# A hybrid encoder layer with seven more fused weight pairs, x loaded once, and x added to the output by accumulating transfers

## The chip, the cores and the metric

The kernel runs on one core of a Trainium2 chip. Its engines are named as in the profile: PE multiplies matrices (PEld is its weight load), DVE works on vectors, ACT does activations and copies, POOL and SP issue transfers here. The metric is the device time of one execution in microseconds; lower is better.

## The reference, cut to what matters

One layer on x of 256 rows and 4096 columns, float32. Its two large products are with w_in (4096 x 14336) and w_out (4096 x 4096).

```python
xn = rms_norm(x, norm_g[l])
h = jnp.einsum('bsd,de->bse', xn, w_in[l])
c_val, c_glu, c_gate, q, k, v, a_gate = jnp.split(h, split_pts, axis=-1)
conv_out = conformer_conv(c_val, c_glu, conv_w[l], conv_b[l], conv_ln_g[l], conv_ln_b[l])
conv_out = conv_out * jax.nn.silu(c_gate)
q = rms_norm(q.reshape(B, S, ATTN_HEADS, HEAD_DIM), q_norm_g[l])
k = rms_norm(k.reshape(B, S, ATTN_HEADS, HEAD_DIM), k_norm_g[l])
attn = longnet_mixture(q, k, v, rel_bias).astype(x.dtype).reshape(B, S, ATTN_WIDTH)
attn_out = attn * jax.nn.silu(a_gate)
mixed = jnp.concatenate([conv_out, attn_out], axis=-1)
x = x + jnp.einsum('bse,ed->bsd', mixed, w_out[l])
```

`conformer_conv` is a gated product, a 31-tap convolution along the rows, a LayerNorm over channels and a swish. The attention has 16 heads of 128 over the 256 rows.

## The kernel before, in words

**Groups and slots.** The weights are read once, in 18 groups of 1024 columns: groups 0 to 13 multiply the normalised x with w_in (four for the convolution, two for its gate, eight for attention), groups 14 to 17 multiply the mixed rows with w_out. A group goes through its 4096 weight rows in 16 pairs of 128, one pair in a slot; `ORDERS` gives the order of the pairs in a group. A pair's 128 x 2048 numbers (1 MB) arrive in one of three `raw` buffers (`load_pair`, on SP's queue).

**Split products.** Both operands are split into a high and a low part of a faster format. ACT makes the high part by a cast, DVE the low part by a subtraction, and PE forms high x high, low x high and high x low. A pair consists of 2 x 2 blocks on each side, so a plain pair (`split_plain`, `plain`) has 8 block products of 3 matmuls, 24 matmuls.

**Fused pairs.** The pairs listed in `FUSED` use a scheme of 7 block products, so 21 matmuls (`split_fused`, `fused`). They need sums of weight blocks, made by DVE in place in `raw` (L1083, L1095, L1096), and sums of the rows' blocks (`block_sums`), made once a pair of rows and kept. Their products go to four more accumulators, m1, m5, m6 and m7, which `add_more` combines behind the group's last fused pair; L1291 to L1309 are its additions in the output groups. The lists give 5, 7, 7, 7, 7 and 6 fused pairs in groups 2 to 7, four in group 14 and seven each in groups 15 to 17.

**Accumulators.** There are two sets of four, `acc` and `side`, which change roles from group to group: a group's m1 to m7 take the set in which the group before kept its outputs.

**Order of the work.** The program is written out by a planner. Every engine runs its instructions in order. `before` issues the split steps of the coming weights as far as there is room (four tiles of 2048 columns, and four of 1024 around fused pairs, `W_SLOTS` and `W_MORE`). Everything else stands in lanes of generators (convolution, attention heads, LayerNorm, the split of the mixed rows), and `pump` lets a lane issue its next step while a budget of DVE and ACT time, credited as PE's matmuls are issued, is above zero. The last slot of a group is plain and sums accumulator by accumulator (`plain_last`: four high matmuls, then two low ones, for each); in slots ahead of it sixteen matmuls with the high half come before the low half.

**The normalisation.** Group 0 multiplies the raw x times the gain g; its root mean square is applied when its outputs leave the accumulators (L876, L878), and group 1 does the same (L901, L907). For it x is loaded a second time in another layout in eight chunks (`load_x`), squared on ACT with a sum along the row (`square_x`), and the reciprocal root (`finish_rstd`) goes through DRAM to become a row that all partitions hold. During group 1 the columns of x are loaded a third time, scaled by that row (L294), cast (L301), subtracted (L303) and from group 2 on used.

**The outputs.** In an output group x is loaded in slot 7 (`xr`, L1156), DVE adds the combined products and then the four accumulators to it (L855), and SP stores it (L857), all at the end of the same group.

Of the kernel before, what the change touches and what calls it, by code (L numbers as in the profile page):

```python
# [132 lines left out]
def layer_kernel(  # L133
# [37 lines left out]
    def rsqrt(src, shape, mul, eps, name, wait=True):  # L171
# [3 lines left out]
        v = sb.tile(shape, F32, tag=tag, bufs=bufs, name=name + "v")  # L175
        r = sb.tile(shape, F32, tag=tag, bufs=bufs, name=name + "r")
        t = sb.tile(shape, F32, tag=tag, bufs=bufs, name=name + "t")
# [74 lines left out]
    def new_split(k, nm):  # L252
        h = sb.tile([P, S], F32R, tag="xh", bufs=KT, name=f"{nm}h{k}")
        l = sb.tile([P, S], F32R, tag="xl", bufs=KT, name=f"{nm}l{k}")
        return h, l

    ss = const.tile([P, 2, 8], F32, name="ss")
    xT, x_chunks = {}, {}

    def load_xT(k0, n, queue):  # L260

        t = t4(f"xT{k0}")
        queue.dma_start(
            t[:, :n, :].rearrange("p a b -> p (a b)"),
            x_cols[:, KT + S * k0 : KT + S * (k0 + n)],
        )
        for i in range(n):
            xT[k0 + i] = t[:, i, :]

    def load_x(c):  # L270
        t = t4(f"x{c}").rearrange("p a b -> p (a b)").rearrange("p (s d) -> p s d", s=2)
        nc.sync.dma_start(t, xs[:, :, 512 * c : 512 * c + 512])
        x_chunks[c] = t

    def square_x(c, s):
        junk = t2(f"junk{c}_{s}")
        nc.scalar.activation(
            junk, x_chunks[c][:, s, :], AF.Square, accum_out=ss[:, s, c : c + 1]
        )

    def split_x(k):
        h, l = new_split(k, "x")
        src = xT.pop(k)
# [7 lines left out]
    def split_xn(k):  # L291

        src = xT[k]
        nc.vector.scalar_tensor_tensor(  # L294
# [16 lines left out]

    split_gens = deque()

    def split_more():

        for gen in list(split_gens)[:4]:
            cost = next(gen, None)
# [1125 lines left out]
```

## Time and profile before

| | before |
|---|---|
| median of 3 runs | 1565.15 us (1565.12 to 1566.41) |
| profiled execution | 1565.9 us, its span 1564.1 us |
| busy: PE, DVE, ACT, POOL | 1559.1, 1335.1, 971.0, 98.9 us |
| matmul records | 6874 |
| group 0 | 0 to 93.8 us |
| group 1 | 93.8 to 180.8 us |
| groups 15 and 16 | 1313.0 to 1395.3 and 1395.3 to 1477.6 us |
| last matmul starts | 1559.9 us |

The span runs from the first to the last instruction. In a row of a view by groups stand the line, the engine, the operation, the tiles written and read, the count, busy time and mean, and after the bar the time for which the engine idled just ahead of these instructions, with what ended it. A busy PE is not PE at its peak: a matmul record lasts 389 ns while the next one starts 227 ns after it.

### The profile page before, as it was taken

The numbers are of one execution on the slowest core, as the hardware profiler recorded it, in microseconds if no ns is written. First come the engines' busy times: TensorE is split into PE (matmuls) and PEld (weight loads), VectorE is DVE, ScalarE is ACT, GpSimd is POOL, SyncE is SP. The second block draws the span as 40 slices with busy tenths as digits, with TensorE's granted clock in tenths as the row PEclk, the third lists the DMA queues.
The fourth block names the chain that finished last, engine by engine and source line by source line (L and its number), as shares of the span: only waits on it lengthen the run. The fifth ranks groups of instructions, "written<-read, shape, count | busy, mean of one in ns | idle before, by whom it ended". The sixth has DMA issues, their size and how long they took to land.

```text
span 1564.1 us, 18620 instructions
## 1 busy us (share of the span) xinstructions
PE 1559.1 (100%) x6874; PEld 1290.6 (83%) x6874; DVE 1335.1 (85%) x1495; ACT 971.0 (62%) x1503; POOL 98.9 (6%) x184
## 2 busy tenths in 40 slices
PE   9999999999999999999999999999999999999999
PEld 7888888888888888888888888888888888888887
DVE  5658898999999999898798898789575888999988
ACT  6755555565556566667776786776557754555453
POOL 0000000000000000001130022021010400000000
PEclk9999999999999999999999999999999999999999
DMA  9768565655656555659686488567674965666663
GB/s 373 293 220 298 189 224 206 226 191 201 233 212 228 199 207 213 216 190 284 219 279 216 174 256 269 194 206 272 220 239 161 282 233 201 239 240 242 223 248 122
DMA packets 64523, 357.22 MB, mean 228 GB/s; under 512 B 9104, under 2 KB 11920, under 8 KB 27824
## 3 DMA queue, kind: packets, MB, share of 16 engines
q1 hardware_dynamic: 54096, 326.38, 59.1%
q0 software_dynamic: 10048, 29.37, 6.3%
q8 instruction: 54, 0.88, 0.2%
q10 hardware_dynamic: 288, 0.28, 0.1%
q14 instruction: 37, 0.30, 0.1%
HBM read 337.09 MB, written 18.91 MB: 228 GB/s over the span
## 4 chain that ended last, share of the span: by engine, by line
PE 99%; DMA 0%; DVE 0%; SPq 0%; ACT 0%; DVEq 0%; issue 0%
PE c L1253 44%; PE c L1255 22%; PE m L1224 6%; PE c L1269 4%; PE m L1226 3%; PE c L1271 2%; PE c L1114 2%; PE c L1112 2%; PE c L1224 2%; PE c L1113 2%; PE acc L956 2%; PE acc L953 2%; PE acc L954 2%; PE m L1114 1%; PE c L1226 1%; PE m L1113 1%
## 5 line engine op out<-in xcount | busy, mean ns | idle before, releaser
L1057 DVE TENSOR_TENSOR wl<-raw,wh 128x2048 fp32r<-128x2048 f32 x208 | 475.7, 2289 | 150.2 <-ACT wh L1051 140.9
L1051 ACT CAST wh<-raw 128x1024 fp32r<-128x1024 f32 x416 | 414.9, 1048 | 222.1 <-PE c L1255 134.7
L1253 PE MATMUL c<-wh,nh 128*128 128x512 f32 x1128 | 439.6, 390 | 0.0
L1255 PE MATMUL c<-wh,nl 128*128 128x512 f32 x1128 | 438.9, 389 | 0.0
L1074 ACT CAST t<-raw 128x1024 fp32r<-128x1024 f32 x128 | 134.9, 1054 | 253.9 <-DVE raw L1083 190.5
L1253 PE MATMUL c<-wl,nh 128*128 128x512 f32 x1128 | 280.5, 391 | 0.0
L1253 PEld LDWEIGHTS c<-wh,nh 128*128 128x128 f32 x1128 | 211.7, 188 | 44.0
L1255 PEld LDWEIGHTS c<-wh,nl 128*128 128x128 f32 x1128 | 211.7, 188 | 44.0
L1253 PEld LDWEIGHTS c<-wl,nh 128*128 128x128 f32 x1128 | 211.8, 188 | 43.9
L1075 DVE TENSOR_TENSOR t<-raw,t 128x1024 fp32r<-128x1024 f32 x128 | 156.2, 1221 | 3.6 <-ACT t L1074 0.3
L508 ACT ACTIVATE cp<-a,wT 128x241 f32<-128x241 f32 (+8 forms) x252 | 105.6, 490 | 6.4 <-DVE cT L537 6.3
L1253 PE MATMUL c<-wh,mh 128*128 128x512 f32 x280 | 109.1, 390 | 0.0
L1255 PE MATMUL c<-wh,ml 128*128 128x512 f32 x280 | 108.9, 389 | 0.0
L546 DVE SCALAR_TENSOR_TENSOR cT<-a,wT,cT 128x255 f32<-128x255 f32 (+7 forms) x228 | 95.1, 473 | 0.5
L1083 DVE TENSOR_TENSOR raw<-raw 128x1024 f32<-128x1024 f32 x64 | 78.4, 1225 | 2.2
L1075 DVE TENSOR_TENSOR b<-raw,b 128x1024 fp32r<-128x1024 f32 x64 | 78.0, 1218 | 0.3
L537 DVE TENSOR_TENSOR cT<-cT,cp 128x964 f32<-128x964 f32 (+8 forms) x63 | 73.8, 1172 | 2.8 <-DVE cT L537 0.5
L1253 PE MATMUL c<-wl,mh 128*128 128x512 f32 x280 | 69.2, 389 | 0.0
L1074 ACT CAST b<-raw 128x1024 fp32r<-128x1024 f32 x64 | 67.0, 1047 | 1.9 <-DMA raw<-in_w_dram 1.2
L1255 PEld LDWEIGHTS c<-wh,ml 128*128 128x128 f32 x280 | 52.6, 188 | 10.9
L1253 PEld LDWEIGHTS c<-wl,mh 128*128 128x128 f32 x280 | 52.6, 188 | 10.9
L1253 PEld LDWEIGHTS c<-wh,mh 128*128 128x128 f32 x280 | 52.6, 188 | 10.9
(343 smaller groups left out, 2275.0 us busy)
## 6 DMA issues: line engine op xcount, KB each, us to landing
raw<-in_w_dram SPq DMA_DIRECT2D x286, 1024.0 KB, 4.9
xT<-in_x_cols_dram SPq DMA_DIRECT2D x15, 512.0 KB, 7.3
x<-in_x_dram SPq DMA_DIRECT2D x8, 512.0 KB, 8.2
xr<-in_x_dram SPq DMA_DIRECT2D x8, 512.0 KB, 6.7
out_dram<-xr SPq DMA_DIRECT2D x15, 256.0 KB, 7.4
T<-bias_dram SPq DMA_DIRECT2D x16, 192.0 KB, 5.6
raw<-in_w_dram SPq DMA_DIRECT2D x3, 512.0 KB, 6.7
turn_qk0d<-turn_qk POOLq DMA_DIRECT2D x2, 512.0 KB, 5.1
```

The source lines that it names most:

```text
L508: nc.scalar.activation(cp[:, t, lo:hi], a[:, t, lo + sh : hi + sh], AF.Copy, scale=wT[:, 4 * cb + t, k : k + 1],)
L537: nc.vector.tensor_add(c[:, :, lo:hi], c[:, :, lo:hi], cp[:, :, lo:hi])
L546: nc.vector.scalar_tensor_tensor(c[:, t, lo:hi], a[:, t, lo + sh : hi + sh], wT[:, 4 * cb + t, k : k + 1], c[:, t, lo:hi], op0=ALU.mult, o ...
L1051: nc.scalar.copy(h, raw_tiles[u][:, k])
L1057: nc.vector.tensor_sub(l, src, h.bitcast(F32))
L1074: nc.scalar.copy(h, src)
L1075: nc.vector.tensor_sub(l, src, h.bitcast(F32))
L1083: nc.vector.tensor_add(r[:, 0:4:3, :], r[:, 0:3:2, :], twice(r[:, 3, :]))
L1224: nc.tensor.matmul(acc, ah, b, start=begin, stop=end)
L1253: nc.tensor.matmul(acc, a[s][0], b[e], start=begin, stop=False)
L1255: nc.tensor.matmul(acc, a[s][1], b[e], start=False, stop=False)
L1269: nc.tensor.matmul(acc, a[s][0], b[e], start=False, stop=end)
```

## The change: what it does

**More fused pairs.** Group 1 gets three (slots 6, 8 and 12), group 2 six, group 7 seven, groups 15 and 16 eight each with a new slot order. In these two the slots run plain, plain, fused, plain, fused, plain, fused, fused, plain, fused, plain, fused, plain, fused, fused, plain. Group 17 keeps its order and its seven.

**x loaded once.** The columns of x stay in eight tiles. ACT squares them whole, DVE adds the squares up, and PE sums over partitions by a product with a tile of ones, which leaves the row in every partition; two one-column products give the same numbers as columns. The pairs of rows are scaled, cast and subtracted (now two blocks in one instruction) from step n = 19 of group 0 on, as far as the budget allows, and group 1 works on normalised rows like the others. The block sums for pairs that group 1 does not fuse are made in group 2.

**Wider or moved operations.** The convolution's centre tap goes from DVE to ACT (`center_gen`). The gate product and the split of the mixed rows work on wider tiles.

**Outputs of groups 14 to 16.** `add_more` combines the fused products in a tile of its own, as in the input groups, with four DVE additions instead of eight; then POOL issues two transfers that add x to that tile as they land. The four accumulators are added, and the result is stored, after slot 0 of the next group (`late_out`). Group 17 keeps the old way.

```diff
+LATE = 0
...
-XN_LOAD = {1 + (5 * c + 1) // 2: c for c in range(8)}
-XN_SQUARE = {n + 5 + s: (c, s) for n, c in XN_LOAD.items() for s in range(2)}
+
+X_LOAD = {0: 12, 1: 16, 3: 20, 5: 24, 6: 28}
+X_SQUARE = {4: 4, 5: 0, 6: 8, 7: 12, 8: 16, 9: 20, 10: 24, 11: 28}
+
+N_SPLIT, N_WAIT = 10, 3
...
-FUSED_IN = range(2, 8)
-N_FUSED = dict(zip(FUSED_IN, (5, 7, 7, 7, 7, 6)))
-FUSED = [(2, 4, 6, 8, 10, 12, 13)[: N_FUSED.get(g, 0)] for g in range(N_IN)]
-SUMS = max(FUSED)
-FUSED += [range(4)] + 3 * [range(7)]
+FUSED_IN = range(1, 8)
+SUMS = (2, 4, 6, 8, 10, 12, 13)
+FUSED = [SUMS if g in FUSED_IN else () for g in range(N_IN)]
+FUSED[1], FUSED[2] = (6, 8, 12), SUMS[1:]
+FUSED += [range(4), range(8), range(8), range(7)]
 ORDERS = N_IN * [range(16)]
 ORDERS += [(4, 5, 8, 9, 10, 11, 12, 13, 0, 14, 1, 15, 2, 6, 3, 7)]
-ORDERS += 3 * [(8, 9, 0, 10, 1, 11, 2, 12, 3, 13, 4, 14, 5, 6, 15, 7)]
+ORDERS += 2 * [(8, 9, 0, 10, 1, 11, 2, 3, 12, 4, 13, 5, 14, 6, 7, 15)]
+ORDERS += [(8, 9, 0, 10, 1, 11, 2, 12, 3, 13, 4, 14, 5, 6, 15, 7)]
...
+    def new_pair(j, nm):
+
+        return [
+            sb.tile([P, 2, S], F32R, tag=f"x{part}", bufs=n_pairs, name=f"{nm}{part}{j}")
+            for part in "hl"
+        ]
...
+    x_tiles = {}
+
+    def sum_squares():
+
+        total = t4("squares")
+        for i, k0 in enumerate(X_SQUARE.values()):
+            t = t4(f"sq{k0}") if i else total
+            if k0:
+                nc.scalar.activation(t, x_tiles[k0], AF.Square)
+            else:
+                nc.scalar.activation(t[:, 0, :], xT[0], AF.Square)
+                nc.scalar.activation(t[:, 1:, :], x_tiles[0][:, :3, :], AF.Square)
+            spend(0, 1055)
+            yield
+            if i:
+                nc.vector.tensor_add(total, total, t)
+                spend(1225)
+        total = flat(total)
+        for n in (512, 256):
+            nc.vector.tensor_add(total[:, :n], total[:, :n], total[:, n : 2 * n])
+            spend(160 + n)
+        yield
+        yield
+        yield from finish_rstd(total[:, :S])
...
+    def split_xn(j):
+
+        steps = 2 * j, 2 * j + 1
+        for k in steps:
+            nc.vector.scalar_tensor_tensor(
+                xT[k], xT[k], g_cols[:, k : k + 1], state["rstd_row"], op0=ALU.mult, op1=ALU.mult
+            )
+            yield 480
...
+        h, l = new_pair(j, "n")
+        for i, k in enumerate(steps):
+            nc.scalar.copy(h[:, i, :], xT[k])
+        yield 0, 800
+        for _ in range(N_WAIT):
+            yield 0
+        if both(j):
+            nc.vector.tensor_sub(l, both(j), h.bitcast(F32))
+            yield 690
+        else:
+            for i, k in enumerate(steps):
+                nc.vector.tensor_sub(l[:, i, :], xT[k], h[:, i, :].bitcast(F32))
+            yield 830
+        for i, k in enumerate(steps):
+            xnh[k], xnl[k] = h[:, i, :], l[:, i, :]
+        if j in FUSED[FUSED_IN[0]]:
+            yield from x_sums(j)
...
+    def split_more(forced=False):
+
+        for gen in list(split_gens)[: 2 if forced else N_SPLIT]:
+            if left[0] <= 0 and not forced:
+                break
             cost = next(gen, None)
             if cost is None:
                 split_gens.remove(gen)
             else:
                 spend(*(cost if isinstance(cost, tuple) else (cost,)))
+
+    def x_sums(j):
+        yield from block_sums(
+            j, src_of=xT, parts=(xnh, xnl), out=xsum, name="xs", small=j in SUMS[5:]
+        )
...
+    def finish_rstd(total):
+
+        pm = side("rms")
+        nc.tensor.matmul(pm[:, :S], ones, total, start=True, stop=True)
+        for i in range(2):
+            nc.tensor.matmul(
+                pm[:, S + i : S + i + 1], total[:, P * i : P * i + P], ones[:, 0:1],
+                start=True, stop=True,
+            )
+        yield
+        steps = rsqrt(pm[:, : S + 2], [P, S + 2], CW / D, NORM_EPS, "rx", wait=False)
+        cost = next(steps)
+        state["held"] -= 1
+        yield cost
+        r = yield from steps
+        state["rstd_row"] = r[:, :S]
+        state["rstd"] = [r[:, S + i : S + i + 1] for i in range(2)]
...
+    def center_gen(cb):
+
         while cb not in aT:
             yield
         a = aT[cb]
         c = t4(f"cT{cb}")
         for t in range(4):
             ch = 4 * cb + t
...
+            nc.scalar.activation(
+                c[:, t, :], a[:, t, :], AF.Identity, bias=col("conv_b", ch),
...
+    xr_tiles, late_out = {}, deque()
...
-        elif g == 1 and e == 1:
-            tile_, first = plain_tiles[(g, 0)]
-            t = first[:, s, :]
-            nc.vector.scalar_tensor_tensor(
-                t, acc, state["rstd"][s], t, op0=ALU.mult, op1=ALU.mult
-            )
-            spend(745)
         else:
-            scale = state["rstd"][s] if g == 1 else 1.0
-            nc.scalar.activation(t, acc, fn, scale=scale)
+            nc.scalar.activation(t, acc, fn)
             spend(0, 620)
...
-            if g == 1:
-                rows = xh, xl
...
-                if g == 1 and slot % 2 == 0 and slot < n_pairs - 2:
-                    load_xT(2 * slot + 4, 4, nc.sync)
-                if slot == 7 and into:
+                if slot == 7 and last_group:
...
-                    if g == 1:
-                        split_gens.extend(split_xn(k) for k in (2 * j, 2 * j + 1))
+                    if g > n_in and slot == LATE:
+                        while late_out:
+                            add_out(*late_out.popleft())
                     continue
...
-                        if into:
+                        if into and not last_group:
+                            late_out.append((g, e, s, acc))
+                        elif into:
                             end = last_group and (s, e) == (1, 1)
                             add_out(g, e, s, acc, (nc.scalar, nc.sync) if end else (nc.sync,))
                         else:
...
-                if g == 1:
-                    split_gens.extend(split_xn(k) for k in (2 * j, 2 * j + 1))
...
+            last_group, into = g == NG - 1, groups[g][0] == "out"
+            if last_group:
...
-            if not into:
+            if not last_group:
                 nc.vector.tensor_sub(r[0][1], more["m5"], u)
                 nc.vector.tensor_sub(r[1][1], more["m5"], v)
                 spend(1375)
+                for e in range(2 if into else 0):
+                    c = groups[g][2 + e]
+                    xr_tiles[(g, e)] = t = more_tiles[(g, e)][1]
+                    nc.gpsimd.dma_start(t, xs[:, :, c : c + 512], accum_op=ALU.add)
                 yield True
                 return
...
+    square_steps, n_xn = sum_squares(), 0
...
         if g > 0:
+            split_gens.extend(split_xn(j) for j in range(n_xn, n_pairs))
+            n_xn = n_pairs
+            if g == FUSED_IN[1]:
+                split_gens.extend(x_sums(j) for j in (*SUMS[1:], SUMS[0]) if j not in FUSED[1])
             stream.group(g)
             continue
...
-            if n % 4 == 0 and 12 + n < KT:
-                load_xT(12 + n, 4, nc.sync)
-            if n == KT - 4:
-                load_xT(0, 4, nc.sync)
-            if n in XN_LOAD:
-                load_x(XN_LOAD[n])
-            if n in XN_SQUARE:
-                square_x(*XN_SQUARE[n])
+            if n in X_LOAD:
+                x_tiles[X_LOAD[n]] = load_xT(X_LOAD[n], 4, nc.sync)
+            if min(X_SQUARE) <= n < KT - 4:
+                next(square_steps, None)
...
+            if "rstd_row" in state:
+                split_gens.extend(split_xn(j) for j in range(n_xn, (n - 1) // 2))
+                n_xn = max(n_xn, (n - 1) // 2)
```

More of the change, by code (lines that the diff above doesn't have):

```diff
@@ L352, in by_block @@
     def by_block(ap):
+        if len(ap.shape) == 3:
+            return ap.rearrange("p t (s a i) -> p (t s) a i", s=2, a=4)
         return ap.rearrange("p (s a i) -> p s a i", s=2, a=4) if len(ap.shape) == 2 else ap
-    def finish_rstd():
-        tot = const.tile([P, 2], F32, name="sstot")
-        nc.vector.reduce_sum(tot, ss, axis=AX.X)
-        r = yield from rsqrt(tot, [P, 2], 1.0 / D, NORM_EPS, "rx", wait=False)
-        keep = const.tile([P, 2], F32, name="rstd")
-        nc.vector.tensor_copy(keep, r)
-        state["rstd"] = [keep[:, s : s + 1] for s in range(2)]
-        flat = tc.dram_tile([2, P], F32, name="rstd_dram")
-        for s in range(2):
-            nc.sync.dma_start(flat[s, :].rearrange("(p o) -> p o", o=1), keep[:, s : s + 1])
-        row = const.tile([P, S], F32, name="rstd_row")
-        nc.sync.dma_start(
-            row, bass.AP(tensor=flat.tensor, offset=flat.offset, ap=[[0, P], [1, S]])
-        )
-        state["rstd_row"] = row
+    def finish_rstd(total):
[5 more added lines that the diff above has]
+                start=True, stop=True,
+            )
+        yield
[6 more added lines that the diff above has]
+        state["rstd"] = [r[:, S + i : S + i + 1] for i in range(2)]
     gqk = const.tile([P, 1], F32, name="gqk")
@@ L462, in near, with far_view @@
         return t
+    def far_view(tile_):
+        return flat(tile_).rearrange("p (a t s i) -> p (t s) a i", a=4, t=4, s=2)
     def turned(tile_):
-        v = flat(tile_).rearrange("p (a t s i) -> p t s a i", a=4, t=4, s=2)
-        return [v[:, t] for t in range(4)]
+        v = far_view(tile_)
+        return [v[:, 2 * t : 2 * t + 2] for t in range(4)]
     a_dram = {}
@@ L523, in conv_gen @@
             ch = 4 * cb + t
-            nc.vector.tensor_scalar(
-                c[:, t, :], a[:, t, :], wT[:, ch, MID : MID + 1], col("conv_b", ch),
-                op0=ALU.mult, op1=ALU.add,
-            )
-            yield 410
-        cT[cb] = c
+            nc.scalar.activation(
+                c[:, t, :], a[:, t, :], AF.Identity, bias=col("conv_b", ch),
+                scale=wT[:, ch, MID : MID + 1],
+            )
+            if t % 2:
+                yield 0, 1020
+        yield from settled()
+        conv_first[cb] = c
+    def conv_gen(cb):
+        while cb not in conv_first:
+            yield
+        a = aT[cb]
+        cT[cb] = c = conv_first[cb]
         order = sorted((k for k in range(TAPS) if k != MID), key=lambda k: abs(k - MID))
@@ L840, in more_rows @@
         if split_gens:
[L841 removed]
+            split_more(True)
         else:
@@ L887, in evacuate_sum @@
         fused = (g, e) in more_tiles
-        if not fused and s == 0 and (g, e) != (1, 1):
+        if not fused and s == 0:
             plain_tiles[(g, e)] = half_tile(g, e)
-        tile_, pair = (more_tiles if fused else plain_tiles).get((g, e)) or plain_tiles[(g, 0)]
+        tile_, pair = (more_tiles if fused else plain_tiles)[(g, e)]
         t = pair[:, s, :]
```

120 lines of the change are left out of this document (45 added, 75 removed).

## The prediction

> **What bounds the kernel now.** I read the page first: the span, the busy shares and the chain of work that ended last.
>
> ```profile
> span 1564.1 us, 18620 instructions
> PE 1559.1 (100%) x6874; PEld 1290.6 (83%) x6874; DVE 1335.1 (85%) x1495; ACT 971.0 (62%) x1503; POOL 98.9 (6%) x184
> ...
> PE 99%; DMA 0%; DVE 0%; SPq 0%; ACT 0%; DVEq 0%; issue 0%
> ```
>
> The chain runs on PE for 99% of the span. A busy PE can still be a slow one, so the next two views are the chain in order of time, for the pace, and the waits of the weight loads, for stalls.
>
> ```profile
> 97.79 2.04 PE c L1253 x9
> ...
> PEld acc L953 <- ACT wh L1026: 0.7, 2, 0.4
> PEld acc L956 <- DVE wh L1027: 0.5, 1, 0.5
> PEld acc L954 <- DVE xl L285: 0.3, 1, 0.3
> PEld acc L953 <- ACT xh L284: 0.3, 1, 0.3
> PEld c L1269 <- DVE wl L1057: 0.2, 1, 0.2
> ```
>
> Nine matmuls take 2.04 us, so one costs 226.7 ns. Behind the warm-up products these are all the waits, 2.0 us in sum, and only one of them, 0.2 us, lies outside group 0 (the tile c; group 0 writes acc). So PE is saturated from end to end: a matmul taken away is worth 226.7 ns, and any other engine matters only where it makes PE wait.
>
> How near DVE is to doing that is read by stages: the first two groups, and the two output groups whose slot order changes (columns: window, its length, then PE, PEld, DVE, ACT busy).
>
> ```profile
> 0.00:93.80 93.80, 92.58 (x406) 76.19 (x407) 56.33 (x78) 64.49 (x107) 0.20 (x4) 1.00 0.82 312
> 93.80:180.80 87.00, 87.00 (x385) 72.05 (x384) 65.15 (x95) 44.05 (x66) 2.87 (x5) 1.00 0.73 253
> ...
> 1313.00:1395.30 82.30, 82.30 (x364) 68.16 (x364) 77.16 (x73) 42.90 (x48) 0.00 (x0) 1.00 0.63 230
> 1395.30:1477.60 82.30, 82.30 (x364) 68.15 (x363) 76.45 (x74) 43.07 (x48) 0.00 (x0) 1.00 0.64 231
> ```
>
> DVE has 37.5 us free in group 0 and 21.9 us in group 1, but only 5.1 us and 5.9 us in output groups 15 and 16. What fills and what idles it there, by groups of instructions in the window of group 15:
>
> ```profile
> L1057 DVE TENSOR_TENSOR wl<-raw,wh 128x2048 fp32r<-128x2048 f32 x10 | 22.8, 2288 | 4.0 <-ACT wh L1051 4.0
> L1075 DVE TENSOR_TENSOR t<-raw,t 128x1024 fp32r<-128x1024 f32 x14 | 17.1, 1221 | 0.4
> L1083 DVE TENSOR_TENSOR raw<-raw 128x1024 f32<-128x1024 f32 x7 | 8.6, 1225 | 0.2
> L1075 DVE TENSOR_TENSOR b<-raw,b 128x1024 fp32r<-128x1024 f32 x7 | 8.5, 1217 | 0.0
> L1095 DVE TENSOR_TENSOR raw<-raw 128x512 f32<-128x512 f32 x7 | 4.8, 693 | 0.2
> L1096 DVE TENSOR_TENSOR raw<-raw 128x512 f32<-128x512 f32 x7 | 4.8, 692 | 0.2
> L1094 DVE TENSOR_TENSOR b<-raw,b 128x512 fp32r<-128x512 f32 x7 | 4.8, 683 | 0.0
> L855 DVE TENSOR_TENSOR xr<-xr,c 128x512 f32<-128x512 f32 x4 | 2.5, 676 | 0.0
> ...
> L1309 DVE TENSOR_TENSOR xr<-xr,vs 128x512 f32<-128x512 f32 x2 | 1.4, 683 | 0.0
> ```
>
> A fused pair costs DVE 2 x 1.221 + 1.225 + 1.217 + 0.693 + 0.692 + 0.683 = 6.95 us while PE needs 21 x 0.2267 = 4.76 us. A plain pair costs 2.29 us against 24 x 0.2267 = 5.44 us. Each plain pair behind a fused one also makes DVE wait for ACT's casts (4.0 us over six such changes, 0.67 us each). So DVE loses lead over PE on every fused pair and regains it on every plain one. How much lead is left at the tightest place stands in the timeline, at the second of two adjacent fused pairs (slot 13 of group 15):
>
> ```profile
> 1381.10 2.43 DVE L1075 TENSOR_TENSOR t<-raw,t 128x1024 fp32r<-128x1024 f32 x2
> 1384.19 4.49 DVE L1057 TENSOR_TENSOR wl<-raw,wh 128x2048 fp32r<-128x2048 f32 x2 [0.67 <-ACT wh L1051]
> ...
> 1383.76 0.84 PE L1224 MATMUL m<-t,msp 128*128 128x512 f32 x3
> ```
>
> The low halves are ready at 1383.53. The third of those matmuls, 2 x 0.2267 after 1383.76, at 1384.21, is the first to read the last of them: 0.7 us of lead. DVE is almost the bound in these groups already.
>
> **The change part by part.**
>
> Matmuls removed. The lists give 39 + 4 + 21 = 64 fused pairs before, and 3 + 6 + 5 x 7 = 44, plus 4 + 8 + 8 + 7 = 27, so 71 after. Seven pairs lose 3 matmuls each: 21 x 0.2267 = -4.76 us on PE, the path that sets the end.
>
> Matmuls added, for the mean of squares: one fp32 product 256 columns wide and two of one column. Their nearest rows are the fp32 score products:
>
> ```profile
> 741.29 3.45 PE psc L717 x16
> ...
> L717 PEld LDWEIGHTS psc<-qk,near_q 128*128 128x128 f32 x64 | 12.1, 189 | 1.8
> ```
>
> Sixteen records take 3.45 us, 0.216 each, and the 32 score products made 64 records, so each is two passes. The wide one costs 2 x 0.216 = 0.43 us. The narrow ones, four passes, have no row: they stream next to nothing (0) or cost a whole such pass each (4 x 0.216 = 0.86). I take their weight loads, 4 x 0.189 = 0.76, as each needs a fresh one. Together +1.2 us, between 0.4 and 1.3. The Trainium skill, page "TensorE: Matmul & The Clock Gate", section "Wait — 56ns, not 53.3ns?", puts the floor between starts of small matmuls at about 25 ns; by that the four cost 0.1 us (an estimate from the page) and this term is 0.5 in place of 1.2.
>
> Extra DVE work in groups 0 and 1. The squares become 7 additions of 1024 columns, two folds, and a 258-column reciprocal root. Rows for these from the LayerNorm that does the same, and for the row scaling:
>
> ```profile
> L570 DVE TENSOR_TENSOR sq<-sq,sq 128x1024 f32<-128x1024 f32 x3 | 3.7, 1222 | 0.1
> ...
> L187 DVE RECIPROCAL rcr<-rcr x1: 1744/1744/1744, 1146.5 to 1146.5; 128x256 f32<-128x256 f32 x1
> L188 DVE TENSOR_TENSOR rct<-rcr x1: 425/425/425, 1148.3 to 1148.3; 128x256 f32<-128x256 f32 x1
> ...
> L294 DVE SCALAR_TENSOR_TENSOR xT<-xT,first_x,rstd_row x32: 472/477/484, 104.9 to 252.4; 128x256 f32<-128x256 f32 x32
> L301 ACT CAST nh<-xT x32: 393/402/407, 109.5 to 254.5; 128x256 fp32r<-128x256 f32 x32
> ```
>
> That is 7 x 1.22, folds of about 0.68 and 0.43, then 1.74 + 5 x 0.425: some 13.5 us in the 37.5 free. The steps put the finished rstd at n = 19 of 32; a step is 12 x 0.2267 = 2.72 us, so 13 steps, 35 us, are left before group 1. One pair of rows costs DVE 2 x 0.477 + 0.68 (512 columns, as L1094) = 1.63 us, so the remaining 24 us could hold most of the sixteen pairs; each needs nine pumps, one a step, so about five are finished when group 1 starts and the others keep ahead of one pair per 5.44 us. Three fused pairs in group 1 cost DVE 3 x 4.66 = 14.0 us more and their evacuation some 5, inside the 21.9 us free, and row work done in group 0 leaves it. So 0 us, hidden behind PE's products; if the cover went, the bare chain is priced as a rival.
>
> The x loads removed (8 chunks and 8 reloads) and the ACT-made centre tap, pair-wide splits and gate products take DMA, DVE or ACT time that is under PE. They cost and save nothing on the path. ACT gains squares and taps of a few us each at 62% busy. More DVE room before the convolution ends matters only if the mixed rows come late for group 14, where PE waited for nothing.
>
> Output groups 15 and 16. Swapping one plain pair for a fused one adds 6.95 - 2.29 = 4.66 us to DVE and takes 0.68 from PE. Adding x by transfer takes four of twelve additions away: -4 x 0.683 = -2.73. DVE busy becomes 77.16 + 4.66 - 2.73 = 79.1 us, with the 4.0 us waiting for casts (again six changes from fused to plain) 83.1 us. PE's group is 82.3 - 0.7 = 81.6 us. DVE is short by 1.5 us a group. Where it shows: slots 13 and 14 are fused and slot 15 is the last plain pair. Its low half is read after 4 matmuls (0.9 us), not after 16 as in another slot, and its split (2.29 us behind the 0.67 us wait) starts only after the last fused split. Bounds: if half the 4.0 us vanish because DVE is late anyway, 0; if the other 1.1 us of idle stay too, 2.6. I take 1.5 in each group, +3.0 in all, since the leftover lead of 0.7 us leaves nothing to spend. Group 14 keeps its slots and loses four additions; group 17 keeps both.
>
> The accumulating transfers. Two of 512 KB a group go out on POOL's queue, which is empty there (POOL 0.00 in both windows), after the last subtraction. Deferred additions in the next group's slot 0 wait for their landing, and behind them in DVE's queue stands the rest of the first fused split, which PE needs; behind the outputs on SP's queue stand weight loads. DVE has, between the subtractions and the deferred additions, two plain low halves and the first three steps of a fused split: 2 x 2.29 + 6.95 - 1.22 = 10.3 us. The nearest landings:
>
> ```profile
> xr<-in_x_dram SPq DMA_DIRECT2D x8, 512.0 KB, 6.7
> ...
> turn_qk0d<-turn_qk POOLq DMA_DIRECT2D x2, 512.0 KB, 5.1
> qk<-turn_qk0d POOLq DMA_DIRECT2D x8, 128.0 KB, 11.8
> ...
> turn_a0d<-turn_a POOLq DMA_DIRECT2D x1, 512.0 KB, 10.4
> ```
>
> Same bytes from the same tensor, 6.7 us; on POOL's queue 5.1 to 11.8. Between 5.1 and twice 6.7 = 13.4 (the tile is read as well) I take 9, nearest to the plain load plus a queue of two: hidden, 0 us. The page "DMA: Bandwidth & Descriptors" of the Trainium skill, section "Anatomy of one DMA — SWDGE (gpsimd) path", fits 2.0 us plus bytes/436e3; 1 MB then takes 4.4 us (an estimate). The 512 KB rows here are slower than that, and by either the additions would not wait.
>
> **Sum.** -4.76 + 1.2 + 3.0 = -0.6 us. The profiled execution took 1565.9 us with a span of 1564.1, so 1.8 us lie around it, untouched; the median of three is 1565.15. Forecast: 1564.6 us, and with its own bounds (stalls 0.8 to 2.6 a group, product 0.4 to 1.3) -2.8 to +1.7: 1562.4 to 1566.9.
>
> **The rivals.** *No stall*: DVE makes up the 1.5 us from its waits for casts. For it: 5.1 us of idle in the window, of which only four are tied to casts. Against: the 0.7 us of lead at the tightest slot with one fused pair fewer. It gives -4.76 + 1.2 = -3.6: 1561.6 us, with the cheap product 1560.8.
>
> *The accumulating transfer lands late* (the slower side). At 13.4 us DVE waits 13.4 - 10.3 = 3.1 us at the start of groups 15, 16 and 17, and with no lead PE pays each: 9.3 us, so 1573.9. It decides from about 11.5 us on, where three waits of 1.2 lift the sum over +0.2%. For it: 11.8 and 10.4 us on the same queue; against: 6.7 and 5.1.
>
> *Rows late in group 1*: the chain (root, scaling, cast, subtraction) now stands ahead of group 1, where before the first scaling came at 104.9, inside it. If rstd slips past about n = 30, PE waits for one bare chain, 2 x 0.477 + 2 x 0.40 + 0.68 and the hand-overs, 3 to 5 us: 1567.6 to 1569.6. Against it: 11 steps of margin, 30 us.
>
> **How the numbers follow.** Forecast 0.46, no stall 0.32, late landing 0.14, late rows 0.08. A measurement of this kernel tells about 0.2% (3.1 us) from no change, so faster means under 1562.0 and slower over 1568.3. Faster: no stall but for a remnant of 0.02, plus 0.02 of the forecast's lower end, 0.32. Slower: late landing, and most of late rows, 0.21. The rest, 0.47, is no change. The range runs from the cheap end of no stall, 1560.9, to late rows, 1568.6; left out are most of the late landings and a little below.
>
> **What would show it.** Right: 21 fewer fp32r matmul records and six more fp32 ones; PE's pace still 226.7 ns; idle of PE's weight loads at the last plain pair of groups 15 and 16 waiting for the low half, 1 to 2 us each; DVE busy near 79 us in these windows. Wrong: no such idle (then 1561.6); DVE waiting for DMA at the deferred additions; PE waiting for the normalised rows near 95 us; or a fused group that ran without stalls before and now stalls.

## The result and the profile after

The kernel after takes 1571.56 us, median of 5 runs (1571.22 to 1575.43), against 1565.47 us (5 runs) for the kernel before on the same chip: a ratio of 1.0045, 95% interval 1.0034 to 1.0056. It is slower by about 6 us. I had forecast 1564.6 with a range up to 1568.6, so the time lies outside it.

The page of the kernel after (span, busy shares, chain of work that ended last):

```profile
span 1571.8 us, 18582 instructions
...
PE 1559.6 (99%) x6859; PEld 1287.3 (82%) x6859; DVE 1365.7 (87%) x1481; ACT 987.7 (63%) x1502; POOL 106.4 (7%) x190
...
PE 90%; DVE 4%; DMA 3%; issue 1%; ACT 1%; POOL 0%; DVEq 0%; SPq 0%; ACTq 0%; POOLq 0%
```

PE ran 6859 products, 15 fewer than before: 21 taken away and six added, as counted. But the chain, which was PE for 99%, now runs through DVE, DMA and ACT for 8% of the span. The waits of PE's weight loads say where (weight load and tile, what it waited for; us in total, times, longest):

```profile
PEld c L1330 <- DVE wl L1121: 3.2, 2, 1.6
PEld m L1285 <- ACT t L1138: 2.8, 4, 0.9
PEld m L1285 <- DVE out L927: 2.4, 2, 2.0
PEld po L831 <- issue: 2.3, 1, 2.3
```

The first row is the last plain pair (the tile c) of groups 15 and 16, waiting for its low half; the second is fused pairs in the same groups, waiting for their weight sums; the third is the first fused pair waiting for the deferred additions, which still hold the PSUM banks that it writes. The fourth, in group 11, is head 7's output product. The windows of groups 15, 16 and 17 (window, its length, then PE, PEld, DVE, ACT, POOL busy):

```profile
1314.10:1400.40 86.30, 83.04 (x361) 67.19 (x360) 78.19 (x73) 44.43 (x49) 3.53 (x4) 1.00 0.64 219
1400.40:1485.20 84.80, 83.03 (x362) 67.21 (x362) 76.76 (x73) 44.52 (x50) 2.39 (x4) 1.00 0.64 223
1485.20:1567.30 82.10, 82.10 (x364) 67.89 (x363) 74.53 (x73) 40.85 (x45) 1.35 (x2) 1.00 0.60 207
```

Without a stall the first two would be 82.3 - 0.68 = 81.6 us each. They lost 4.7 and 3.2 us; in group 17, which starts with deferred additions as well, PE is busy for all of its 82.10 us. What DVE waited for at these additions, from its timeline (start, us, idle before and its releaser), and from the list by source line of the accumulating transfers:

```profile
1313.08 0.68 DVE L1361 TENSOR_TENSOR out<-m,out 128x512 f32<-128x512 f32 x1
...
1323.91 1.28 DVE L927 TENSOR_TENSOR out<-out,c 128x512 f32<-128x512 f32 x2
...
1328.67 1.28 DVE L927 TENSOR_TENSOR out<-out,c 128x512 f32<-128x512 f32 x2 [3.49 <-DMA out<-in_x_dram]
...
1413.43 1.28 DVE L927 TENSOR_TENSOR out<-out,c 128x512 f32<-128x512 f32 x2 [1.91 <-DMA out<-in_x_dram]
...
1497.73 1.28 DVE L927 TENSOR_TENSOR out<-out,c 128x512 f32<-128x512 f32 x2 [1.48 <-DMA out<-in_x_dram]
```

```profile
DMA to landing us min/median/max: 5.8/9.5/13.4
```

The additions to the first half of the columns find x landed, those to the second half do not, in all three groups. Between the end of the last subtraction (1313.76) and the first addition lie 10.15 us of cover, and 11.4 us until DVE is free for the additions to the second half (1325.19). The second transfer took up to 13.4 us from its issue; it had landed when DVE's wait ended at 1328.67, 14.9 us after the subtraction.

Head 7, in the timeline of POOL and then in that of PE, of the kernel after:

```profile
963.30 0.56 POOL L455 DMA_DIRECT2D turn_p7d<-T  x1
...
972.17 2.17 POOL L462 DMA_DIRECT2D pr<-turn_p7d  x4 [6.10 <-PE po L831]
```

```profile
970.05 2.75 PE L831 MATMUL po<-pr,agv 128*128 128x256 f32 x12
980.14 1.10 PE L831 MATMUL po<-pr,agv 128*128 128x256 f32 x4 [1.86 <-DMA pr<-turn_p7d]
```

and both of the kernel before:

```profile
963.51 0.56 POOL L404 DMA_DIRECT2D turn_p7d<-T  x1
...
971.93 2.17 POOL L411 DMA_DIRECT2D pr<-turn_p7d  x4 [5.65 <-ACT wh L1051]
```

```profile
971.04 2.75 PE L762 MATMUL po<-pr,agv 128*128 128x256 f32 x12
982.75 1.02 PE L762 MATMUL po<-pr,agv 128*128 128x256 f32 x4
```

POOL turns head 7's probabilities at the same time in both, to 0.3 us. PE asks for them earlier: before, 11.7 us after the products of the three other heads (971.04); now, taking off the 2.3 us that the weight load waits, 7.8 us after them (970.05). This product has moved forward in the order of PE's work, and its transfer has not moved with it.

So four things could be behind the 6 us: the accumulating transfers land late, DVE is short of time in groups 15 and 16, head 7 is late, or the input part costs something not seen here. The runs below take them apart. In the diffs, lines that are only re-indented are left out, and three dots stand for other lines left out.

### The profile page after: what moved, and what is told of

Same layout as the page of the kernel before. It is cut to its first block, busy times and chain, and to the rows that moved or that the text cites. A ratio compares the mean times of both kernels' runs of the same rounds, so it can differ in the third digit from the quotient of the medians.

```text
span 1571.8 us, 18582 instructions
## 1 busy us (share of the span) xinstructions
PE 1559.6 (99%) x6859; PEld 1287.3 (82%) x6859; DVE 1365.7 (87%) x1481; ACT 987.7 (63%) x1502; POOL 106.4 (7%) x190
## 4 chain that ended last, share of the span: by engine, by line
PE 90%; DVE 4%; DMA 3%; issue 1%; ACT 1%; POOL 0%; DVEq 0%; SPq 0%; ACTq 0%; POOLq 0%
PE c L1314 40%; PE c L1316 20%; PE m L1285 5%; PE c L1330 4%; PE m L1287 3%; PE c L1332 2%; PE c L1285 2%; DMA out<-in_x_dram 2%; PE c L1177 2%; PE c L1178 2%; PE c L1176 2%; PE acc L1017 2%; PE acc L1018 2%; PE acc L1020 2%; PE psc L786 1%
## 5 line engine op out<-in xcount | busy, mean ns | idle before, releaser
L1121 DVE TENSOR_TENSOR wl<-raw,wh 128x2048 fp32r<-128x2048 f32 x201 | 459.8, 2289 | 141.8 <-ACT wh L1115 136.7
L1314 PE MATMUL c<-wh,nh 128*128 128x512 f32 x1208 | 471.1, 390 | 0.0
L1316 PE MATMUL c<-wh,nl 128*128 128x512 f32 x1208 | 470.1, 389 | 0.0
L1314 PE MATMUL c<-wl,nh 128*128 128x512 f32 x1208 | 299.8, 390 | 0.0
L1314 PEld LDWEIGHTS c<-wh,nh 128*128 128x128 f32 x1208 | 226.8, 188 | 47.3
L1139 DVE TENSOR_TENSOR t<-raw,t 128x1024 fp32r<-128x1024 f32 x142 | 173.2, 1222 | 3.4 <-ACT t L1138 0.6
L563 ACT ACTIVATE cp<-a,wT 128x241 f32<-128x241 f32 (+9 forms) x260 | 108.6, 489 | 5.8 <-DVE cT L603 5.8
L612 DVE SCALAR_TENSOR_TENSOR cT<-a,wT,cT 128x255 f32<-128x255 f32 (+8 forms) x220 | 91.2, 475 | 0.6
L603 DVE TENSOR_TENSOR cT<-cT,cp 128x964 f32<-128x964 f32 (+9 forms) x65 | 76.1, 1170 | 1.9
L1285 PE MATMUL m<-t,xsp 128*128 128x512 f32 x186 | 62.3, 389 | 0.0
L1316 PEld LDWEIGHTS c<-wh,ml 128*128 128x128 f32 x264 | 49.6, 188 | 10.3
L1314 PEld LDWEIGHTS c<-wh,mh 128*128 128x128 f32 x264 | 49.6, 188 | 10.3
```

The lines of the kernel that those rows point to most:

```text
L563: nc.scalar.activation(cp[:, t, lo:hi], a[:, t, lo + sh : hi + sh], AF.Copy, scale=wT[:, 4 * cb + t, k : k + 1],)
L603: nc.vector.tensor_add(c[:, :, lo:hi], c[:, :, lo:hi], cp[:, :, lo:hi])
L612: nc.vector.scalar_tensor_tensor(c[:, t, lo:hi], a[:, t, lo + sh : hi + sh], wT[:, 4 * cb + t, k : k + 1], c[:, t, lo:hi], op0=ALU.mult, o ...
L1121: nc.vector.tensor_sub(l, src, h.bitcast(F32))
L1139: nc.vector.tensor_sub(l, src, h.bitcast(F32))
L1285: nc.tensor.matmul(acc, ah, b, start=begin, stop=end)
```

## The experiments

**x left out of the output.** Theory A: DVE is short by about 1.2 us a group, and the late landing is the rest. x is not added in groups 14 to 16.

```
-   nc.gpsimd.dma_start(t, xs[:, :, c : c + 512], accum_op=ALU.add)
```

> The changed kernel without the accumulating transfers of x in groups 14 to 16: x is left out of these 3072 output columns. The changed kernel stands at 1571.6 us, with PE stalls of 4.7 and 3.1 us in groups 15 and 16. Theory A (DVE is short there, by 1.5 us a group as forecast, and the late landing of x adds the rest): the waits for x go, about 1.5 us a group stay at the last plain pair, 1566.6 us. Theory B (the late landing alone: without it DVE keeps up): no stall in either group, 1563.7 us. Theory C (short DVE alone, the wait for x only takes the place of other idle time): unchanged, 1571.6 us.

1565.72 us (1565.27 to 1567.86), ratio to before 1.0002 (0.9992 to 1.0011). The waits of its weight loads:

```profile
PEld c L1330 <- DVE wl L1121: 2.5, 2, 1.2
PEld po L831 <- DMA pr<-turn_p7d: 2.0, 1, 2.0
```

The waits at deferred additions and fused pairs are gone, the last plain pair keeps 1.2 us a group, head 7 keeps its stall. Theory A. The fused pairs' own waits (2.8 us above) came with the transfers and go with them.

**Plain transfers in place of accumulating ones**, on the same queue, at the same time, with the same bytes. x then overwrites the fused products in the output tiles of groups 14 to 16.

```
-   nc.gpsimd.dma_start(t, xs[:, :, c : c + 512], accum_op=ALU.add)
+   nc.gpsimd.dma_start(t, xs[:, :, c : c + 512])
```

> The changed kernel with plain transfers in place of the accumulating ones, same bytes, tile, queue and place in the program; x then overwrites the combined products of the fused pairs, which are left out of the output. If the accumulation itself is slow, the second transfer of a group lands in about 7 us, as other loads of x, in place of 13, DVE's waits for x vanish, and the time is that of the run without x. If the queue and the weight stream beside it are slow, it lands at 12 to 13 us again and the time stays at 1571.6 us.

1566.02 us (1565.1 to 1566.87), ratio 1.0001 (0.9992 to 1.001); again only 1.2 us a group at the last plain pair. The transfers in the window 1300 to 1345 (POOL's queue: packets, MB, share of 16 engines; then the issues, KB each, median us to landing), plain:

```profile
q0 software_dynamic: 288, 1.05, 6.7%
...
out<-in_x_dram POOLq DMA_DIRECT2D x2, 512.0 KB, 4.5
```

and accumulating, in the kernel after:

```profile
q0 software_dynamic: 544, 1.05, 13.8%
...
out<-in_x_dram POOLq DMA_DIRECT2D x2, 512.0 KB, 9.7
```

The queue is not slow and the bytes are not many: accumulating is slow. The same 1.05 MB goes out in nearly twice the packets and holds the DMA engines twice as long.

**Seven fused pairs in groups 15 and 16, in the order of before**, with accumulating transfers and deferred additions kept (69 pairs).

```
- FUSED += [range(4), range(8), range(8), range(7)]
+ FUSED += [range(4)] + 3 * [range(7)]
- ORDERS += 2 * [(8, 9, 0, 10, 1, 11, 2, 3, 12, 4, 13, 5, 14, 6, 7, 15)]
- ORDERS += [(8, 9, 0, 10, 1, 11, 2, 12, 3, 13, 4, 14, 5, 6, 15, 7)]
+ ORDERS += 3 * [(8, 9, 0, 10, 1, 11, 2, 12, 3, 13, 4, 14, 5, 6, 15, 7)]
```

> The changed kernel with seven fused pairs and the old slot order in groups 15 and 16 (69 fused pairs); accumulating transfers and deferred additions stay. PE gets 6 matmuls back, +1.4 us; DVE loses 2 x 4.66 us of work. Theory A: no stall for lack of DVE time, and most of the 3.5 and 1.9 us of waiting for x falls on regained lead: 1565 to 1567 us. Theory B: the waits for x cost PE what they did, 7.9 us: about 1573 us. Theory C: no stalls at all, 1565.0 us.

1567.08 us (1565.96 to 1572.47), ratio 1.0014 (1.0005 to 1.0023).

```profile
PEld po L830 <- issue: 2.8, 1, 2.8
PEld m L1284 <- DVE out L926: 1.6, 1, 1.6
```

Theory A is the nearest: the median lies just above its 1565 to 1567 us, with head 7's stall in it, and far from theory B's 1573. The stall at the last plain pair is gone; in this order two plain pairs end the group, where the changed one has two fused pairs ahead of the last plain one. The wait for the deferred additions stays once, at 1.6 us, in group 15; in group 16 PE shows none. There DVE doesn't wait for x either: its second low half waits 4.24 us for ACT's cast, the additions start only at 1408.14, and the second transfer, issued at about 1395.4, took 10.8 us.

**The input part alone**: groups 14 to 17 as in the kernel before, 69 pairs.

```
  (FUSED and ORDERS as in the last diff)
- if slot == 7 and last_group:
+ if slot == 7 and into:
- if into and not last_group:
-     late_out.append((g, e, s, acc))
- elif into:
+ if into:
- if last_group:
+ if into:
      r = [[xr_tiles[(g, e)][:, s, :] for e in range(2)] for s in range(2)]
...
- if last_group:
+ if into:
      for s in range(2):
          nc.vector.tensor_add(r[s][1], r[s][1], more["m5"])
...
- if not last_group:
+ if not into:
      nc.vector.tensor_sub(r[0][1], more["m5"], u)
```

> The input part of the change alone: x loaded once, wider operations, 44 fused input pairs, but the outputs as before (x loaded in slot 7, eight DVE additions, additions at the end of the group, seven fused pairs, old order). 5 fused pairs more than before, -3.4 us, the mean of squares on PE +1.3. Theory A, B and C alike: no stall in the output groups, 1563.3 to 1564 us. The rival, that the input part has a cost of its own (start of group 0, a late head near 978 us): 1565.5 us or more.

1565.6 us (1564.7 to 1570.14), ratio 1.0007 (0.9999 to 1.0016): the rival. Its 15 products fewer, 3.4 us, bring nothing. One large wait is left in the profiled execution, which took 1568.56 us, 3 us more than the median:

```profile
PEld po L830 <- issue: 3.1, 1, 3.1
```

This stall costs more than its length. From PE's timeline, and the window behind the stall (its length, then PE, PEld, DVE, ACT, POOL busy, the granted clock, DMA):

```profile
980.05 2.04 PE L830 MATMUL po<-pr,agv 128*128 128x256 f32 x4 [2.71 <-DMA pr<-turn_p7d]
980.00:984.00 4.00, 3.94 (x11) 3.19 (x12) 3.96 (x5) 1.66 (x4) 0.00 (x0) 0.60 0.30 45
```

Behind the 2.7 us in which PE idled, the granted clock is 0.60 over these 4 us. They hold 11 products; the 10 us from 990 on, at clock 1.00, hold 46. The four products of head 7 take 2.04 us, in the kernel after 1.10. In the kernel after and in the runs without x and with seven fused pairs, where PE idled 1.9, 1.6 and 2.4 us, the clock stays at 1.00 in this place. The execution is 4.5 us longer than the median of the next run, which has no such stall: 3.1 us of wait and about 1.4 us behind it (an estimate from the two times). The three longest executions, 1569.27 to 1570.14 us, have a mean granted clock of 0.997 or 0.998, the seven shortest 1.000 and at most 1565.9 us, so the same may have happened there; of those there is no trace.

**The input part alone, head 7 held back.** The product of head 7 waits 6 us of planned time more, so that its transfer is hidden again.

```
+ if h == 7:
+     yield from settled()
+     yield from settled()
  while hg not in mixA or not state["side"]:
```

> Only the input part of the change, groups 14 to 17 as before (69 fused pairs), and head 7's output product held back by two settling times (6 us of planned time), so that its turned probabilities have landed when PE gets there. Theory A (the input part costs 1.3 us for the fp32 products and well under 1 us of small gaps, saves 5 x 3 x 0.2267 = 3.4 us, and the only large stall is head 7's at 977): without that stall the time is 1563.2 to 1564.1, and the long runs near 1569 go with it. Rival B (the stall is only the place where a general lateness of the input part shows, or the wider splits and loads cost PE elsewhere): 1565.3 or more, with a new stall in another place.

1564.09 us (1563.93 to 1564.7), ratio 0.9989 (0.998 to 0.9998): faster than both kernels. Outside group 0 one wait of PE's weight loads is left:

```profile
PEld c L1179 <- DVE xsp12l L390: 0.4, 1, 0.4
```

PE does the products that came behind head 7's first, and nothing waits for them; the stall was a matter of order. It ate 1.5 us of the input part's gain by the medians, and 4.5 us or more in four of the eleven executions. The top end of the runs fell from 1570.14 to 1564.7 with it.

**The whole change, head 7 held back** (the same three lines in the kernel after).

> The whole change with head 7's output product held back by 6 us of planned time. Theory A: 1571.6 - 2.2 = 1569.4 (1568.8 to 1569.8), the stalls of groups 15 and 16 unchanged at 4.7 and 3.1 us. Rival B: PE gets its time back at the next wait, 1571 or more.

1570.72 us (1570.28 to 1570.95), ratio 1.0032 (1.0019 to 1.0044). Less than expected: the median falls by 0.8 us, not 2.2, though the profile loses the whole wait. The profiled execution of the kernel after took 1573.54 us, 2 us more than its median, so its 2.3 us of wait may be more than the others pay; of those there is no trace. In the profiled executions of the other kernels with this input part the same wait is 0.4 us (plain transfers), 2.0, 2.8 and 3.1, so it is not one fixed cost. The 0.8 us are near the noise too: the two ratios' intervals overlap, though every execution with head 7 held back (at most 1570.95) is shorter than every one without (at least 1571.22). Groups 15 and 16 stall as before:

```profile
PEld c L1333 <- DVE wl L1124: 3.3, 2, 1.6
PEld m L1288 <- ACT t L1141: 3.0, 4, 0.9
PEld m L1288 <- DVE out L930: 2.5, 3, 1.8
```

From here on, head 7 is held back in every kernel, and 1570.72 us is what they are compared with.

**One accumulating transfer a group in place of two**; x is left out of the other half of the columns.

```
- nc.gpsimd.dma_start(t, xs[:, :, c : c + 512], accum_op=ALU.add)
+ if e == 0:
+     nc.gpsimd.dma_start(t, xs[:, :, c : c + 512], accum_op=ALU.add)
```

> The whole change with head 7 held back, and only the first of the two accumulating transfers of each group (x is left out of the other half of the columns of groups 14 to 16). Theory A (the two transfers run one behind the other at some 6 us each, so it is the second that is late): the one lands within 6 to 9 us, under the 10.2 us of cover, and only the 1.2 us a group at the last plain pair stay: about 1564.2. Rival B (one accumulating transfer alone takes 13 us beside the weight stream): the stalls stay, 1568 to 1569.4.

1565.08 us (1564.76 to 1565.82), ratio 0.9996 (0.9987 to 1.0005). The landing, in its list by source line:

```profile
DMA to landing us min/median/max: 5.9/5.9/5.9
```

Alone, an accumulating transfer lands in 5.9 us each time, as the first of two does (5.8 to 6.1), and nothing waits for it. So it is the second that is late, and that fits theory A, one behind the other. That is not all of it: in the kernel after it had landed 14.1 us after the first was issued (1314.57 to 1328.67), and twice 5.9 is 11.8. Taking it away is worth 5.64 us; the time is 0.9 us above theory A's, and stalls of 1.3 to 1.4 us a group stay at the last plain pair.

**Deferred additions left out**, the two transfers kept (the products c are missing in groups 14 to 16).

```
- nc.vector.tensor_add(t, t, acc[:, n * i : n * i + n])
+ if g == NG - 1:
+     nc.vector.tensor_add(t, t, acc[:, n * i : n * i + n])
```

> The whole change with head 7 held back, and without the deferred additions of groups 14 to 16 (their products c are left out of the output; the accumulating transfers stay, and the outputs are sent once these have landed). DVE loses 4 x 0.64 = 2.6 us of work a group, and no PSUM bank waits for a landing. Theory A (late landing reaches PE through the deferred additions, and the rest is DVE being 1.2 us short a group): both parts go, groups 15 and 16 run without stalls, 1569.4 - 4.7 - 3.1 = 1561.6. Rival B (the stall at the last plain pair belongs to its place, its low half read after 4 matmuls, and not to the amount of DVE work): 1.2 us a group stays, 1564.0. Rival C (the transfers slow PE or the weight stream by their traffic): 1566 or more.

1566.82 us (1565.9 to 1567.9), ratio 1.0007 (0.9999 to 1.0016): not A and not B, and in the range of rival C. The last plain pair still waits, and longer, although DVE has 2.6 us less to do:

```profile
PEld c L1334 <- DVE wl L1125: 3.1, 2, 1.6
```

The timelines of SP and then of ACT at the start of group 15, and the landing of the two weight loads that were issued just ahead of the stores, show two reasons:

```profile
1317.74 9.97 SPq L933 DMA_DIRECT2D out_dram<-out  x4
1327.81 68.27 SPq L253 DMA_DIRECT2D raw<-in_w_dram  x15
```

```profile
1325.61 1.05 ACT L1142 CAST b<-raw 128x1024 fp32r<-128x1024 f32 x1 [2.52 <-DMA raw<-in_w_dram]
...
1333.69 2.00 ACT L1119 CAST wh<-raw 128x1024 fp32r<-128x1024 f32 x2 [1.30 <-DMA raw<-in_w_dram]
```

```profile
DMA to landing us min/median/max: 7.6/8.8/10.0
```

The output stores, which now wait for the landing themselves, stand on SP's queue for 10 us, and the weight loads stand behind them; the cast at 1333.69 waits for one of these. The cast at 1325.61 doesn't: its load was issued ahead of the stores and took 10.0 us. The two loads at this place take 4.7 and 4.8 us in the run without x, 6.5 and 6.6 beside two plain transfers, 6.9 and 7.0 beside one accumulating transfer, and 7.6 and 10.0 beside two. So the accumulating transfers also slow the weight loads, as rival C has it, and the late landing reaches PE through more doors than the deferred additions. How the time divides among them was not measured. This run alone doesn't tell theory A from B, so the next leaves out the transfers too.

**Neither transfers nor deferred additions** (both edits together; x and c are left out of groups 14 to 16).

> The whole change with head 7 held back, without the accumulating transfers and without the deferred additions (groups 14 to 16: x and the products c are left out). DVE has 2.6 us less to do in each group and nothing waits for a landing, neither PSUM banks nor the output stores on SP's queue, behind which weight loads stand. Theory A (the 1.2 us a group at the last plain pair are DVE being short of time in the group): gone, about 1565.1 - 2.4 = 1562.7. Theory B (they belong to the order: two fused pairs, then a plain one whose low half is read after 4 matmuls): 1.2 us a group stay, about 1565.0.

1562.87 us (1562.34 to 1564.12), ratio 0.9981 (0.9972 to 0.9989): theory A, within 0.2 us. Groups 15 and 16 by windows:

```profile
1311.50:1393.10 81.60, 81.60 (x361) 67.57 (x360) 74.51 (x69) 44.78 (x50) 0.00 (x0) 1.00 0.60 219
1393.10:1474.70 81.60, 81.60 (x361) 67.57 (x360) 74.50 (x69) 44.88 (x50) 0.00 (x0) 1.00 0.61 219
```

Both are 81.60 us long and PE is busy all of it. The order with two fused pairs ahead of the last plain one is no obstacle; the additions, which the first run still had, are what DVE can't fit.

**Another order in groups 15 and 16**, x left out as in the first run.

```
- ORDERS += 2 * [(8, 9, 0, 10, 1, 11, 2, 3, 12, 4, 13, 5, 14, 6, 7, 15)]
+ ORDERS += 2 * [(8, 9, 0, 10, 1, 2, 11, 3, 4, 12, 5, 13, 6, 14, 7, 15)]
```

> The whole change with head 7 held back and without the accumulating transfers (x left out of groups 14 to 16), and with another order in groups 15 and 16: the two places with two fused pairs in a row are moved to the middle, so that a plain and a single fused pair stand ahead of the last plain one. The deferred additions stay, and so does DVE's total. Theory A (short of time): the 1.2 us a group stay, at another place perhaps, 1565.0. Theory B (order): no stall at the last plain pair, 1562.7; a stall at the second pair of two fused ones in the middle would speak for A.

1565.25 us (1564.98 to 1565.97), ratio 0.9998 (0.9989 to 1.0007). Theory A: the stall is cut in two and moves, to the second of two neighbours and to the last pair, and its sum stays (3.0 us over both groups, 2.5 in the first run).

```profile
PEld m L1288 <- ACT t L1141: 2.0, 2, 1.0
...
PEld c L1333 <- DVE wl L1124: 1.0, 2, 0.5
```

**All of x, half by one accumulating transfer and half as before** (a plain load, added by DVE), in the changed order and in the other.

```
- if slot == 7 and last_group:
-     for e in range(2):
+ if slot == 7 and into:
+     for e in range(0 if last_group else 1, 2):
...
- for e in range(2):
+ for e in range(1 if into else 2):
      more_tiles[(g, e)] = half_tile(g, e)
...
- if last_group:
+ if into:
      for s in range(2):
          nc.vector.tensor_add(r[s][1], r[s][1], more["m5"])
...
- for e in range(2 if into else 0):
+ for e in range(1 if into else 0):
      (accumulating transfer)
```

> Complete computation, head 7 held back: the first half of x by one accumulating transfer a group, the second half loaded by a plain transfer and added by DVE, as in the kernel before, 2 x 0.68 = 1.4 us more of DVE a group than with one transfer alone. Order as changed. Theory A: 1565.1 + 2 x 1.4 = 1567.8. Theory B (order alone): 1565.1.

> The same with the other order of groups 15 and 16. Theory A: 1567.8, as without it. Theory B: 1562.7, under the kernel with the input part alone (1564.1).

1564.94 us (1564.38 to 1565.44), ratio 0.9995 (0.9986 to 1.0004), and with the other order 1565.08 (1564.84 to 1565.68), ratio 0.9996 (0.9987 to 1.0005). Theory A as I had put it, short of time in the group as a whole, falls here: 1.4 us more of DVE cost nothing. Theory B falls with the other order, for which it gave 1562.7. Nothing is left out of the output in these two, and against 1570.72 us they are 5.8 and 5.6 us faster: the second accumulating transfer is what cost that. The end of group 15 and the start of group 16 in DVE's timeline, with one transfer alone:

```profile
1387.75 2.29 DVE L1124 TENSOR_TENSOR wl<-raw,wh 128x2048 fp32r<-128x2048 f32 x1 [0.67 <-ACT wh L1118]
...
1392.84 2.28 DVE L1124 TENSOR_TENSOR wl<-raw,wh 128x2048 fp32r<-128x2048 f32 x1
1396.57 2.29 DVE L1124 TENSOR_TENSOR wl<-raw,wh 128x2048 fp32r<-128x2048 f32 x1 [1.45 <-ACT wh L1118]
```

and with the added half:

```profile
1387.42 2.29 DVE L1124 TENSOR_TENSOR wl<-raw,wh 128x2048 fp32r<-128x2048 f32 x1 [0.68 <-ACT wh L1118]
1389.63 1.28 DVE L1355 TENSOR_TENSOR xr<-xr,m 128x512 f32<-128x512 f32 x2
...
1393.34 2.29 DVE L1124 TENSOR_TENSOR wl<-raw,wh 128x2048 fp32r<-128x2048 f32 x1
1396.21 2.29 DVE L1124 TENSOR_TENSOR wl<-raw,wh 128x2048 fp32r<-128x2048 f32 x1 [0.58 <-ACT wh L1118]
```

The additions come after the last low half (wl) that PE is waiting for. They put off the next group's first low half by half a microsecond (1393.34 for 1392.84). Its second low half waits for ACT's cast in both kernels, 1.45 us without them and 0.58 us with them, and starts no later (1396.21 for 1396.57): the additions fell into time in which DVE would have waited. That group ends with the same stall, 1.3 us. What counts is DVE's work from this wait to the group's last low half; deferring the additions puts 2.6 us into that stretch, and 1.2 of them don't fit.

## Why the prediction was wrong

**The steps that failed.** The first is "I take 9, nearest to the plain load plus a queue of two: hidden, 0 us". The cover was right (10.3 us worked out, 10.15 measured). The upper bound, 13.4 us, was met by luck: it was a plain load's 6.7 us twice, for reading the tile as well, and one accumulating transfer alone took 5.9. The rows at 5.1 to 6.7 us were near the first transfer's landing (5.8) and the 13.4 was the second's, and the additions wait for both. No choice between them was open: the last landing was the one to hold against the cover. The rival *The accumulating transfer lands late* names the mechanism, the place and the 13.4 us. Its price was too high, since it let PE pay 3.1 us three times: DVE waited 3.49, 1.91 and 1.48 us, less each time, and group 17 hid its part; the second transfer cost 5.64 us, not 9.3. The landing itself was much the same in all three groups (12.8 to 13.4 us), so it is DVE that came later to the additions. The rival also left out that the transfers slow weight loads and hold up the output stores. Its chance of 0.14 was what the step allowed it, and too little.

The Trainium skill's page "DMA: Bandwidth & Descriptors", section "Anatomy of one DMA — SWDGE (gpsimd) path", led the same way: its fit, 2.0 us plus bytes/436e3, gives 3.2 us for 512 KB (an estimate). Here the plain transfers took 4.5 us, an accumulating one alone 5.9 and the second of two up to 13.4; the measurement decides.

The second is "They cost and save nothing on the path", of the x loads, the centre tap and the wider splits. I asked whether the moved work was hidden, not whether the order of everything else stayed. The input part moved head 7's product ahead of its transfer; with that part alone this ate 1.5 us (1565.6 against 1564.09), in the whole change 0.8 us, which is near the noise. Which of its edits moved the product was not tried. None of my rivals had it.

**The steps that held.** The 21 products: 6859 records, and groups 15 and 16 at 81.60 us where nothing stalls, against 82.30 before, 3 x 0.2267 = 0.68 less. The products for the mean of squares, in the timeline of the weight loads:

```profile
46.62 0.42 PEld L408 LDWEIGHTS rms<-squares,ones 128*128 128x128 f32 x2
47.07 0.63 PEld L410 LDWEIGHTS rms<-ones,squares 128*128 128x128 f32 x4
47.62 0.19 PEld L1017 LDWEIGHTS acc<-wh,xh 128*128 128x128 f32 x1
```

From the first of them to PE's next own load 1.00 us pass; I had said 1.2, between 0.4 and 1.3. The four narrow passes take 47.62 - 47.07 = 0.55 us, 0.14 each, less than the 0.19 of a weight load's record. By the floor of about 25 ns between starts, in the Trainium skill's "TensorE: Matmul & The Clock Gate", section "Wait — 56ns, not 53.3ns?", all four would take 0.1 us (an estimate); a floor is only a lower limit, and here it was not the price. *Rows late in group 1* did not happen; the only wait there is 0.4 us for a pair's sums.

**Half right**: the short DVE, +1.5 us a group at the last plain pair. Place and size hold (1.2 us, inside the bounds 0 to 2.6), and *No stall* falls with it. The reason doesn't: I compared DVE's total in a group with PE's, and the run with half of x added by DVE has 1.4 us more in the total and the same stall. It is right about the stretch from the group's second low half to its last. The 0.8 us that the sum takes as the low end of this stall stands on no row; the bounds beside it were 0 to 2.6.

**The sum, by the runs.** 1571.56 us are made up of: 1562.87 with neither transfers nor deferred additions; +2.21 for one transfer and the additions (to 1565.08), where two stalls of 1.3 to 1.4 us show; +5.64 for the second transfer (to 1570.72); +0.84 for head 7, less sure than the others. Against before, the first of these is -2.8 us, where the products alone make -4.76 + 1.00 = -3.8. About 1 us is left, 0.4 of it the wait in group 1; where the rest lies stays open.

## What to carry to other kernels

Where an edit waits for several transfers, hold the landing of the last one against the cover, and price everything that waits for it or runs beside it: here one late transfer held PSUM banks, DVE and the output stores, and behind those weight loads, and it slowed the loads beside it. Work moved on an engine near its limit is cheap or dear by where it lands, in the stretch up to the last thing that the bound engine waits for or in time in which the engine would have waited, not by the engine's total. In a kernel with a written order, an edit far from the path can still move a short step ahead of its data: after any such edit look at each transfer that was hidden before. And look at the granted clock behind a stall of PE: it can cost more than the wait. Seven more fused pairs were worth less here than five with the old output part (1564.09 us against 1570.72, head 7 held back in both).

## What was not expected of the hardware

An accumulating transfer of 512 KB into SBUF took 5.9 us alone and up to 13.4 us as the second of two, beside a weight stream (14.4 in the run without deferred additions), where a plain one on the same queue took 4.5 us (median; 7.8 at most); in a window of 45 us it used 544 packets and 13.8% of the DMA engines against 288 and 6.7% for the same 1.05 MB. Whether the packets' number or the reading of the tile makes it slow was not tried. Weight loads of 1 MB beside two of them took 7.6 and 10.0 us, without any 4.7 and 4.8.

Behind one stall of PE, of 2.7 us, the granted clock was 0.60 over 4 us; behind those of 1.6, 1.9 and 2.4 us it stayed at 1.00. Four cases give no threshold.
